# Causal mask added by VectorE in PSUM instead of by a product, the value halves added by VectorE, and another first weight load

## The chip, the cores and the metric

The kernel runs on one core of one Trainium2 chip. The metric is the device time of one execution in microseconds (us): the median of the runs of a kernel. The notes below call the engines PE (TensorE), DVE (VectorE), ACT (ScalarE), POOL (GpSimd) and SP (SyncE, which issues nearly all DMAs). PEld is TensorE's weight load.

## What is computed

One inference step of a hybrid streaming encoder layer for 1024 new frames of one stream (the prompt) and 32 frames of another that has 512 cached frames. Width 1024, 8 heads of 64, feed-forward width 4096, everything in float32.

```python
def _fox_attend(q, k, v, cq, ck, q_pos, k_pos):
    s = jnp.einsum('bqhd,bkhd->bhqk', q, k).astype(jnp.float32) * ATTN_SCALE
    bias = jnp.swapaxes(cq, 1, 2)[:, :, :, None] - jnp.swapaxes(ck, 1, 2)[:, :, None, :]
    mask = k_pos[None, :] <= q_pos[:, None]
    s = jnp.where(mask, s + bias, NEG_INF)
    p = jax.nn.softmax(s, axis=-1)
    return jnp.einsum('bhqk,bkhd->bqhd', p.astype(v.dtype), v)

u, q, k, v, logf, gc, ga = _in_proj(xp, w_in[l], b_f[l])        # one combined projection
y_conv = _conv_branch(u_ext, w_dw[l], b_dw[l], ln_conv_g[l], ln_conv_b[l], w_conv_out[l])
o_attn = _fox_prompt(q, k, v, logf)                             # blocks of 128 queries
# tail: two gated branches, w_o, LN, feed-forward with relu squared, LN
x1 = _layer_norm(DN_ALPHA * x + mix, ln1_g, ln1_b)
h = jnp.square(jax.nn.relu(jnp.einsum('btd,df->btf', x1, w_up)))
return _layer_norm(DN_ALPHA * x1 + jnp.einsum('btf,fd->btd', h, w_down), ln2_g, ln2_b)
```

## The kernel before

**Products.** Float32 operands are split into a high and a low part (`xh`, `xl`, `whi`, `wlo`), and each product is three: high by high, high by low, low by high. ACT copies the high part into the format that TensorE takes, DVE (in the attention stage POOL, for weights) subtracts it from the original to get the low part.

**Stages.** A first stage projects x to GLU, v, q, k and six of sixteen gate blocks. Then comes the attention, then the two output projections (`ps_yc`, `ps_yo`), `w_o` with a layer norm, and the feed-forward, which takes more than half of the time. Engines PE, DVE, ACT and POOL run their instructions in the order in which the program writes them. SP's order is made by the framework from the same program.

**The start.** `x_stream` loads the first weight block `raw` in halves and x in twelve pieces `xr` of two rows of 128 each (four pieces for each third of the frames). ACT turns them into `whi` and `xh`, DVE makes `wlo` and `xl`. The first block of products, `ps_glub`, goes through all high by high and high by low products in the order of the rows of x and then through the products with `wlo`. Small products that nobody reads (`ps_warm`, from `keep_warm`) run ahead of it and between its first products.

**Attention.** The work is a list of units: eight prompt heads of eight rows (a row is a block of 128 queries, named r = 0 to 7, that sees (r + 1) x 128 keys), and four cached units for the other stream between them. The loop runs a pipeline over these units. In iteration i PE makes the scores of unit i (`scores`, tile `ps_s`), the value products of unit i-3 (`values`, tile `ps_pv`, only at odd r, for two rows at once) and the transposes of unit i-2 (`turn`, tile `ps_tr`). DVE takes the negated maximum `mn` of the new scores (line 961), the reciprocal of the sum of unit i-1, normalises `p` of unit i-1 (line 231) and subtracts the high half from the transposed block (`tl`, unit i-2). ACT copies the high half `th`, and makes the exponential of the scores. There are two buffers for scores.

The mask of the diagonal block is the last product of a score: weights `ident_b` (an identity), moving operand `mask_b` (0 or a very large number, in bfloat16), both slices of the tile `bfs`. After the value products `fold` adds the two halves of the partitions (the parts from the high and the low half of v), and splits the result for the next stage; ACT copies both halves, POOL adds, casts and subtracts:

```python
act(a, pv[0:DH, :parts * n], AF.Copy)
act(b, pv[DH:P, :parts * n], AF.Copy)
tt(a, a, b, ADD, "pool")
```

**What sets the order.** While it writes the program, a planner (class `Issue`) keeps a model of each engine's time. `fill` is called ahead of the scores, transposes and value products: as long as the model says that their inputs aren't ready, and while a quota lasts, it puts in a step of other work (six products of one of the ten remaining gate blocks `ps_g`, or of the first `ps_yc` blocks). The quota begins at 16 steps and grows by 1.7 with each unit; there are 132 steps in all. Other work (`service`) is put in where the model says that it is due. The planner's costs for each instruction stand in the methods of `Issue`.

Of the kernel before, what the change touches and what calls it, by code (L numbers as in the profile page):

```python
# [267 lines left out]
def hybrid_layer(ctx: ExitStack, tc, io):  # L268
# [31 lines left out]
    eps = const.tile([P, 1], F32, name="eps")  # L300
    nc.gpsimd.memset(eps, EPS)
    tiny = const.tile([P, 1], F32, name="tiny")
    act(tiny, eps, AF.Sigmoid)

    def par(name, j):
        return prm[:, PRM[name] + j:PRM[name] + j + 1]
# [17 lines left out]
    class Weights:  # L324
# [1 line left out]
            self.raw, self.parts, self.taken, self.done, self.halves = [], [], 0, 0, 0  # L326
            self.engine, self.limit = "dve", NWO + 1

        def load(self):
            i = len(self.raw)  # L330
            held["raw"] += 1
            self.raw.append(ring.tile([P, RW // 2], F32, tag="raw", bufs=RAWB, name=f"raw{i}"))
            w = plan[i // 2]
            n = w.shape[1] // 2
            dma(self.raw[i][:, :n], w[:, i % 2 * n:(i % 2 + 1) * n])

        def split(self):
            i = self.halves
# [154 lines left out]
    with pool("conv") as pv_, pool("a") as pa, pool("pa", space=PSUM) as psa:  # L493
# [6 lines left out]
        def x_stream():  # L500
            raw = []

            def issue():
                i = len(raw)
                if i < 4 * NCH:
                    r = pa.tile([P, 2, CH], F32, tag="xr", bufs=XB, name=f"xr{i}")
                    dma(r, io["x"][2 * (i % 4):2 * (i % 4) + 2, :, chunks[i // 4]].rearrange("k p t -> p k t"))
                    raw.append(r)

            W.load()  # L510
            issue()
            issue()
            W.load()
            for _ in range(XB - 2):
                issue()
                if len(raw) == 4:
                    W.load()
                    W.load()
            W.split()
            for i in range(4 * NCH):  # L520
                if i == 1:
                    W.split()
                    W.load()
                    W.load()
                yield [raw[i]]
                cs = chunks[i // 4]
                for n in range(2):
                    k = 2 * (i % 4) + n
                    act(xh[k][:, cs], raw[i][:, n, :], AF.Copy)
                    tt(xl[k][:, cs], raw[i][:, n, :], f32(xh[k][:, cs]), SUB)  # L530
                xin.append(i)
                for _ in range((0, 1, 1, 2)[i] if i < 4 else 1):
                    issue()
# [6 lines left out]
        def keep_warm(n):  # L540
            for _ in range(n):
                nc.tensor.matmul(ps_warm, lhsT=warm[:, :P], rhs=warm, start=True, stop=True)
# [41 lines left out]
        def glu(kind, j, c):  # L584
            ps = bank(f"glu{kind}{j}")[:, :CH]
            if (kind, j) not in glu_w:
                glu_w[kind, j] = W.take()
            if (kind, j, c) == ("b", 0, 0):

                terms = on_x(glu_w[kind, j], c)  # L590
                for k, (wh, _, h, l) in enumerate(terms):
                    mm(ps, wh, h, k == 0, False)
                    mm(ps, wh, l, False, False)
                    keep_warm({1: 5, 3: 2}.get(k, 0))
                    I.service()
                for k, (_, wl, h, _) in enumerate(terms):
                    mm(ps, wl, h, False, k == KD - 1)
                I.service()
            else:
                dense(ps, on_x(glu_w[kind, j], c))  # L600
            if kind == "b":
                sig[j, c] = pa.tile([P, CH], F32, tag="sig", bufs=4, name=f"sig{j}_{c}")
                act(sig[j, c], ps, AF.Sigmoid)
            elif c < 2:
                tt(u[j][:, HIST + c * CH:HIST + (c + 1) * CH], ps, sig[j, c], MUL)
            else:
                e = SEQ - 2 * CH
                tt(u[j][:, HIST + 2 * CH:HIST + SEQ], ps[:, :e], sig[j, c][:, :e], MUL)
                tt(u[j][:, UE - DEC:UE], ps[:, e:], sig[j, c][:, e:], MUL)
                dma(io["conv_p"][:, j, :], u[j][:, SEQ:SEQ + HIST])  # L610
                dma(io["conv_d"][:, j, :], u[j][:, UE - HIST:UE])
# [209 lines left out]
    with pool("b") as pb, pool("pb", space=PSUM) as psb:  # L821
# [151 lines left out]
        def fold(pv, n, tag, outs, parts=1, into=None):  # L973
# [1 line left out]
            at = 0 if into is None else into[0]  # L975
            pr = slice(at, at + DH)
            a, b = (pb.tile([P, 256], F32, tag=x, bufs=1, name=f"{x}_{tag}")[pr, :parts * n] for x in ("oa", "ob"))
            act(a, pv[0:DH, :parts * n], AF.Copy)
            act(b, pv[DH:P, :parts * n], AF.Copy)
            tt(a, a, b, ADD, "pool")  # L980
            if parts > 1:
                tt(a[:, :n], a[:, :n], a[:, n:], ADD, "pool")
                a = a[:, :n]
# [14 lines left out]
        class Rows:  # L998
# [5 lines left out]
            def scores(self):  # L1004
                k1, k2, q1, q2, _ = self.ops
                n, tag = self.n, f"{self.h}_{self.r}"
                ps = psb.tile([P, SEQ], F32, tag="s", bufs=2, name=f"ps_s_{tag}")
                qc = slice(self.r * P, (self.r + 1) * P)
                I.fill(k1, k2, q1, q2, ps)
                for a in range(0, n, 512):  # L1010
                    w = min(512, n - a)
                    mm(ps[:, a:a + w], q1[:, qc], k1[:, a:a + w], True, False)
                    mm(ps[:, a:a + w], q2[:, qc], k2[:, a:a + w], False, a + w < n)
                mm(ps[:, n - P:n], ident_b, mask_b, False, True)
                self.sm = softmax_a(ps[:, :n], n, tag)

            def weigh(self):
# [941 lines left out]
```

## Time and profile before

| | |
|---|---|
| median of 3 runs | 1446.77 us (1445.07 to 1447.04) |
| profiled execution, its own time | 1445.13 us |
| its span, first to last instruction | 1443.0 us |
| mean granted TensorE clock over the span | 0.997 of 2.4 GHz |
| PE busy | 1427.9 us, 99% |
| DVE busy | 1121.0 us, 78% |
| ACT busy | 679.1 us, 47% |
| POOL busy | 124.5 us, 9% |
| attention on PE | from 334 to 572 us of the span |

Times within the trace count from the start of the span. A product is shown with a modelled end: products overlap, and the distance from one start to the next is what a product takes of PE. So PE's busy share can't tell whether PE is at its peak, and the starts are what to read.

### The profile page before, as it was taken

Reading aid. Unit: us, or ns where it says so; the run is one execution under the profiler, and the core shown is the slowest. Engines: PE = TensorE matmul, PEld = TensorE weight load, DVE = VectorE, ACT = ScalarE, POOL = GpSimd, SP = SyncE. Lnnn points to the kernel's source line nnn. Section 1 sums busy time; section 2 is a strip of 40 time slices with the busy share of each in tenths; the row PEclk is TensorE's granted clock in tenths of the full one; section 3 lists DMA queues with packets and bytes.
Section 4 is the critical chain, followed back from the end, with each engine's and each line's share of the span. In section 5 each row is a group of like instructions: output and inputs, shape, how many; then the busy total and the mean of one; then the engine's idle time right before and its main releaser. Section 6 shows DMA issues by size and latency. Waiting matters only on the chain.

```text
span 1443.0 us, 28013 instructions
## 1 busy us (share of the span) xinstructions
PE 1427.9 (99%) x10643; PEld 1406.3 (97%) x10643; DVE 1121.0 (78%) x1927; ACT 679.1 (47%) x1426; POOL 124.5 (9%) x183
## 2 busy tenths in 40 slices
PE   9999999999999999999999999999999999999996
PEld 8999999999999999999999999999999999999996
DVE  6999899875666555756697888889876799889668
ACT  5113433455656556533245666676657323322134
POOL 0000000023455533000000000000000000000000
PEclk9999999999999999999999999999999999999998
DMA  7125454278455557425243348766689999894212
GB/s 247 48 61 160 159 171 167 85 244 233 120 150 147 155 146 260 152 93 182 85 138 120 131 152 295 249 241 230 228 283 342 340 321 330 270 324 179 67 45 77
DMA packets 157441, 267.91 MB, mean 186 GB/s; under 512 B 22680, under 2 KB 81272, under 8 KB 157308
## 3 DMA queue, kind: packets, MB, share of 16 engines
q1 hardware_dynamic: 156492, 264.24, 55.0%
q0 software_dynamic: 544, 1.59, 0.5%
q8 instruction: 84, 1.38, 0.4%
q14 instruction: 49, 0.40, 0.1%
q10 hardware_dynamic: 272, 0.29, 0.1%
HBM read 168.29 MB, written 97.74 MB: 184 GB/s over the span
## 4 chain that ended last, share of the span: by engine, by line
PE 97%; DVE 1%; ACT 0%; DMA 0%; issue 0%; SPq 0%; DVEq 0%
PE ps_u L206 18%; PE ps_d L206 17%; PE ps_g L206 13%; PE ps_o L206 6%; PE ps_dn L206 6%; PE ps_up L206 5%; PE ps_v L206 4%; PE ps_yc L206 3%; PE ps_k L206 3%; PE ps_glua L206 3%; PE ps_q L206 3%; PE ps_glub L206 3%; PE ps_yo L206 3%; PE ps_s L206 3%; PE ps_pv L206 2%; PE ps_tr L210 2%
## 5 line engine op out<-in xcount | busy, mean ns | idle before, releaser
L235 DVE SCALAR_TENSOR_TENSOR ca<-u,prm,ca 128x1086 f32<-128x1086 f32 x120 | 161.8, 1348 | 2.4
L206 PE MATMUL ps_g<-xh,whi 128*128 128x352 f32 x384 | 131.8, 343 | 0.0
L218 ACT ACTIVATE swhi<-s 128x512 fp32r<-128x512 f32 x100 | 61.9, 624 | 148.2 <-DVE s L227 139.8
L206 PE MATMUL ps_g<-xh,wlo 128*128 128x352 f32 x384 | 123.8, 322 | 0.0
L206 PE MATMUL ps_g<-xl,whi 128*128 128x352 f32 x384 | 121.5, 322 | 0.0
L206 PE MATMUL ps_u<-tl,swhi 128*128 128x264 f32 x416 | 118.4, 285 | 0.0
L206 PE MATMUL ps_u<-th,swhi 128*128 128x264 f32 x416 | 118.2, 284 | 0.0
L206 PE MATMUL ps_u<-th,swlo 128*128 128x264 f32 x416 | 118.2, 284 | 0.0
L218 ACT ACTIVATE whi<-raw 128x512 fp32r<-128x512 f32 (+1 forms) x120 | 69.7, 624 | 68.6 <-PE ps_glua L206 21.8
L227 DVE TENSOR_TENSOR tl<-ps_tr,th 128x512 fp32r<-128x512 f32 (+2 forms) x96 | 51.5, 553 | 60.1 <-ACT th L218 59.4
L206 PE MATMUL ps_d<-hu_h,swhi 128*128 128x264 f32 x480 | 93.0, 285 | 0.0
L206 PE MATMUL ps_d<-hu_l,swhi 128*128 128x264 f32 x480 | 92.8, 285 | 0.0
L218 ACT ACTIVATE r<-r 128x528 f32<-128x528 f32 (+1 forms) x120 | 73.9, 615 | 37.8 <-DVE r L227 35.5
L227 DVE TENSOR_TENSOR r<-r,ps_u 128x528 f32<-128x528 f32 x91 | 62.7, 701 | 29.5 <-PE ps_u L206 29.5
L227 DVE TENSOR_TENSOR wlo<-raw,whi 128x512 fp32r<-128x512 f32 (+1 forms) x100 | 64.9, 687 | 23.5 <-ACT whi L218 21.6
L206 PEld LDWEIGHTS ps_u<-th,swhi 128*128 128x128 f32 x416 | 78.3, 188 | 0.0
L206 PEld LDWEIGHTS ps_u<-th,swlo 128*128 128x128 f32 x416 | 78.3, 188 | 0.0
L206 PEld LDWEIGHTS ps_u<-tl,swhi 128*128 128x128 f32 x416 | 78.2, 188 | 0.0
L227 POOL TENSOR_TENSOR acc<-acc,lnrest 128x288 f32<-128x288 f32 x4 | 3.0, 796 | 856.7 <-ACT lnrest L218 856.7
L206 PEld LDWEIGHTS ps_d<-hu_h,swhi 128*128 128x128 f32 x480 | 74.6, 189 | 0.3 <-issue 0.2
L206 PEld LDWEIGHTS ps_d<-hu_l,swhi 128*128 128x128 f32 x480 | 74.6, 189 | 0.0
L206 PEld LDWEIGHTS ps_g<-xh,whi 128*128 128x128 f32 x384 | 72.7, 189 | 0.8
(424 smaller groups left out, 5005.5 us busy)
## 6 DMA issues: line engine op xcount, KB each, us to landing
h_s<-sp SPq DMA_DIRECT2D x84, 528.0 KB
raw<-in_w_in_dram SPq DMA_DIRECT2D x64, 256.0 KB
hu_h<-h_s SPq DMA_DIRECT2D x30, 528.0 KB
hu_l<-h_s SPq DMA_DIRECT2D x30, 528.0 KB
sraw<-in_w_up_dram SPq DMA_DIRECT2D x52, 256.0 KB
hu<-h_s SPq DMA_DIRECT2D x24, 528.0 KB
sraw<-in_w_ds_dram SPq DMA_DIRECT2D x48, 256.0 KB
g_s<-gt SPq DMA_DIRECT2D x48, 176.0 KB
```

Of the source, the lines that this page charges most:

```text
L206: self.nc.tensor.matmul(ps, lhsT=w, rhs=x, start=start, stop=stop)
L210: self.nc.tensor.transpose(ps, x, ident)
L218: self.nc.scalar.activation(out, in_, func, **kw)
L227: (self.nc.vector if eng == "dve" else self.nc.gpsimd).tensor_tensor(out, a, b, op)
L235: self.nc.vector.scalar_tensor_tensor(out, a, s, b, op0, op1)
```

## The change

1. In `Rows.scores` the mask is no product any more. The second product of each piece closes the accumulation, and DVE adds `mask_b` to the last 128 columns of the scores in PSUM, ahead of the reduction. 64 products leave PE, 64 additions of 128 x 128 come to DVE. The cached units keep their mask product.
2. In `fold` ACT copies only the lower half `b`, and DVE adds the upper half, read from PSUM, to it. 36 copies leave ACT, 36 additions move from POOL to DVE.
3. The first weight half is issued on ACT's DMA queue, and the dummy activation that loads ACT's table for the sigmoid comes behind it. All other loads stay on SP.
4. In the first stage the second half of the first weight block is split after two pieces of x instead of one, and the two loads behind it move with it.
5. Between the first products there are 3 small warming products instead of 7.

```diff
-    act(tiny, eps, AF.Sigmoid)
...
-        def load(self):
+        def load(self, queue=None):
...
-            dma(self.raw[i][:, :n], w[:, i % 2 * n:(i % 2 + 1) * n])
+            dma(self.raw[i][:, :n], w[:, i % 2 * n:(i % 2 + 1) * n], queue)
...
-            W.load()
+            W.load(nc.scalar)
+            act(tiny, eps, AF.Sigmoid)
...
-                if i == 1:
+                if i == 2:
...
-                    keep_warm({1: 5, 3: 2}.get(k, 0))
+                    keep_warm({1: 2, 3: 1}.get(k, 0))
...
-            act(a, pv[0:DH, :parts * n], AF.Copy)
             act(b, pv[DH:P, :parts * n], AF.Copy)
-            tt(a, a, b, ADD, "pool")
+            tt(a, pv[0:DH, :parts * n], b, ADD)
...
-                    mm(ps[:, a:a + w], q2[:, qc], k2[:, a:a + w], False, a + w < n)
-                mm(ps[:, n - P:n], ident_b, mask_b, False, True)
+                    mm(ps[:, a:a + w], q2[:, qc], k2[:, a:a + w], False, True)
+                tt(ps[:, n - P:n], ps[:, n - P:n], mask_b, ADD)
```

Since the planner's times change, its filling steps in the attention move. Outside the start and the attention the order of all engines stays as it was, and the 132 steps stay inside the attention.

On DVE, in the second head: the iteration that makes the scores of row 4 and the one after it. `mn` is the reduction, `rs` the reciprocal, `p` the normalising, `tl` the low half of the transposed block, `oa` the sum of the halves. Before:

```order
L961 TENSOR_REDUCE mn_4_4177<-ps_s_4_4171 128x1
L239 RECIPROCAL rs_3_4156<-rs_3_4156 128x1
L231 TENSOR_SCALAR p_3_4155<-p_3_4155,rs_3_4156 128x512
L227 TENSOR_TENSOR tl_2_0_4208<-ps_tr_2_0_4209,th_2_0_4207 128x3x128
L961 TENSOR_REDUCE mn_5_4223<-ps_s_5_4217 128x1
L239 RECIPROCAL rs_4_4180<-rs_4_4180 128x1
L231 TENSOR_SCALAR p_4_4179<-p_4_4179,rs_4_4180 128x640
L227 TENSOR_TENSOR tl_2_0_4208<-ps_tr_3_0_4228,th_2_0_4207 128x4x128
```

After:

```order
L227 TENSOR_TENSOR ps_s_4_4185<-ps_s_4_4185,bfs 128x128
L961 TENSOR_REDUCE mn_4_4191<-ps_s_4_4185 128x1
L239 RECIPROCAL rs_3_4170<-rs_3_4170 128x1
L227 TENSOR_TENSOR oa_0_4226<-ps_pv_0_4221,ob_0_4227 64x256
L231 TENSOR_SCALAR p_3_4169<-p_3_4169,rs_3_4170 128x512
L227 TENSOR_TENSOR tl_2_0_4237<-ps_tr_2_0_4238,th_2_0_4236 128x3x128
L227 TENSOR_TENSOR ps_s_5_4246<-ps_s_5_4246,bfs 128x128
L961 TENSOR_REDUCE mn_5_4252<-ps_s_5_4246 128x1
L239 RECIPROCAL rs_4_4194<-rs_4_4194 128x1
```

The mask's addition stands ahead of each reduction; `oa`, which reads the value product and ACT's copy `ob`, stands ahead of the normalising of row 3 and of `tl` of row 2.

On PE, in the third head: from the scores of row 5 to the transposes of row 3. Before:

```order
L206 MATMUL ps_s_5_4596<-k_2_4079,q_2_4080 128x512
L206 MATMUL ps_s_5_4596<-k_0_3563,q_0_3565 128x512
L206 MATMUL ps_s_5_4596<-k_2_4079,q_2_4080 128x256
L206 MATMUL ps_s_5_4596<-k_0_3563,q_0_3565 128x256
L206 LDWEIGHTS bfs
L206 MATMUL ps_s_5_4596<-bfs 128x128
L210 MATMUL ps_tr_3_0_4607<-ident,p_3_4534 128x128 x4
L206 MATMUL ps_g_2_4621<-xh_139,whi_3518 128x352
```

After:

```order
L206 MATMUL ps_s_5_4644<-k_2_4091,q_2_4092 128x512
L206 MATMUL ps_s_5_4644<-k_0_3559,q_0_3561 128x512
L206 MATMUL ps_s_5_4644<-k_2_4091,q_2_4092 128x256
L206 MATMUL ps_s_5_4644<-k_0_3559,q_0_3561 128x256
L206 MATMUL ps_g_0_4579<-xh_144,whi_3672 128x352
L206 MATMUL ps_g_0_4579<-xl_152,whi_3672 128x352
L206 MATMUL ps_g_0_4579<-xh_144,wlo_3673 128x352
L206 MATMUL ps_g_0_4579<-xh_145,whi_3672 128x352
L206 MATMUL ps_g_0_4579<-xl_153,whi_3672 128x352
L206 MATMUL ps_g_0_4579<-xh_145,wlo_3673 128x352
L210 MATMUL ps_tr_3_0_4655<-ident,p_3_4575 128x128 x4
```

The product with `bfs` and its weight load are gone, and a filling step of six gate products, which stood behind the transposes, now stands ahead of them.

On ACT, at the start of the program. Before:

```order
L218 ACT_TABLE_LOAD
L218 ACTIVATE tiny<-eps 128x1
L218 ACTIVATE whi_210<-raw_186 128x512
L218 ACTIVATE xh_139<-xr_188 128x352
L218 ACTIVATE xh_140<-xr_188 128x352
L218 ACTIVATE whi_210<-raw_192 128x512
L218 ACTIVATE xh_141<-xr_190 128x352
L218 ACTIVATE xh_142<-xr_190 128x352
L218 ACTIVATE xh_143<-xr_194 128x352
```

After:

```order
L201 DMA raw_185<-in_w_in_dram 128x512
L218 ACT_TABLE_LOAD
L218 ACTIVATE tiny<-eps 128x1
L218 ACTIVATE whi_210<-raw_185 128x512
L218 ACTIVATE xh_138<-xr_188 128x352
L218 ACTIVATE xh_139<-xr_188 128x352
L218 ACTIVATE xh_140<-xr_190 128x352
L218 ACTIVATE xh_141<-xr_190 128x352
L218 ACTIVATE whi_210<-raw_192 128x512
```

The first DMA is issued by ACT ahead of its table load, and the second half of `whi` comes behind the fourth row of x instead of the second.

## Rows read from the trace of the kernel before

**Rows 1.** The page: span, busy time by engine, and the chain by engine.

```profile
span 1443.0 us, 28013 instructions
...
PE 1427.9 (99%) x10643; PEld 1406.3 (97%) x10643; DVE 1121.0 (78%) x1927; ACT 679.1 (47%) x1426; POOL 124.5 (9%) x183
...
PE 97%; DVE 1%; ACT 0%; DMA 0%; issue 0%; SPq 0%; DVEq 0%
```

**Rows 2.** Busy time in the attention: stretch, length, PE, PEld, DVE, ACT, POOL, clock, DMA.

```profile
334.00:572.00 238.00, 237.00 (x1656) 223.23 (x1656) 147.66 (x316) 147.74 (x370) 106.84 (x145) 1.00 0.58 168
```

**Rows 3.** Instructions that read the mask's tile: count, ns min/median/max, first and last start.

```profile
L206 PE MATMUL ps_s<-bfs x64: 229/230/233, 334.5 to 559.3; 128*128 128x128 bf16 x64
```

**Rows 4.** Timeline of PE, a mask with gate products behind it: start, length.

```profile
338.87 0.23 PE L206 MATMUL ps_s<-bfs 128*128 128x128 bf16 x1
338.91 0.41 PE L206 MATMUL ps_g<-xh,whi 128*128 128x352 f32 x1
339.16 0.32 PE L206 MATMUL ps_g<-xl,whi 128*128 128x352 f32 x1
339.32 0.32 PE L206 MATMUL ps_g<-xh,wlo 128*128 128x352 f32 x1
```

**Rows 5.** Timeline of PE, a mask with transposes behind it.

```profile
341.43 0.23 PE L206 MATMUL ps_s<-bfs 128*128 128x128 bf16 x1
341.49 0.61 PE L210 MATMUL ps_tr<-ident,p 128*128 128x128 f32 x4
```

**Rows 6.** Groups by form in the attention, DVE: busy us, mean ns, idle before.

```profile
L227 DVE TENSOR_TENSOR tl<-ps_tr,th 128x512 fp32r<-128x512 f32 x48 | 32.4, 686 | 27.5 <-ACT th L218 27.5
...
L227 DVE TENSOR_TENSOR tl<-ps_tr,th 128x256 fp32r<-128x256 f32 x16 | 6.6, 414 | 1.2 <-ACT th L218 1.2
...
L227 DVE TENSOR_TENSOR tl<-ps_tr,th 128x128 fp32r<-128x128 f32 x16 | 4.6, 288 | 19.0 <-ACT th L218 18.9
```

**Rows 7.** Instructions on the sum of the halves, ns min/median/max.

```profile
L218 ACT ACTIVATE oa<-ps_pv x32: 363/378/382, 340.6 to 572.0; 64x256 f32<-64x256 f32 x32
L227 POOL TENSOR_TENSOR oa<-oa,ob x32: 723/728/738, 341.4 to 572.9; 64x256 f32<-64x256 f32 x32
```

**Rows 8.** Waits in the attention: who on whom, us in total, times, longest.

```profile
DVE tl L227 <- ACT th L218: 59.4, 41, 3.1
...
PEld ps_s L206 <- ACT p L218: 1.1, 2, 0.9
```

**Rows 9.** Timeline of all engines in the second head, rows 1 to 5.

```profile
365.63 0.49 DVE L231 TENSOR_SCALAR p<-p,rs 128x512 f32<-128x512 f32 x1
...
366.53 0.38 ACT L218 ACTIVATE ob<-ps_pv 64x256 f32<-64x256 f32 x1
...
366.99 0.63 PE L210 MATMUL ps_tr<-ident,p 128*128 128x128 f32 x4
...
369.46 0.68 DVE L227 TENSOR_TENSOR tl<-ps_tr,th 128x512 fp32r<-128x512 f32 x1
...
370.31 0.28 PE L206 MATMUL ps_pv<-th,v 128*128 128x256 f32 x1
```

**Rows 10.** Timeline of the start, all engines, with idle time before and its releaser.

```profile
0.74 0.40 SPq L201 DMA_DIRECT2D raw<-in_w_in_dram  x1
...
1.19 4.11 PE L542 MATMUL ps_warm<-warm 128*128 128x256 bf16 x19 [1.19 <-DVE warm L537]
...
6.88 0.63 ACT L218 ACTIVATE whi<-raw 128x512 fp32r<-128x512 f32 x1 [0.93 <-DMA raw<-in_w_in_dram]
...
7.54 0.69 DVE L227 TENSOR_TENSOR wlo<-raw,whi 128x512 fp32r<-128x512 f32 x1 [0.98 <-ACT whi L218]
...
8.15 2.70 DVE L227 TENSOR_TENSOR xl<-xr,xh 128x352 fp32r<-128x352 f32 x6
```

**Rows 11.** Busy time at the start, columns as in rows 2, last two DMA share and GB/s.

```profile
1.00:2.00 1.00, 0.81 (x4) 0.58 (x5) 0.13 (x1) 1.00 (x1) 0.72 (x8) 1.00 0.15 33
...
3.00:3.50 0.50, 0.50 (x4) 0.32 (x3) 0.00 (x0) 0.00 (x0) 0.00 (x0) 1.00 0.96 246
```

## The prediction

> **What bounds the kernel now.** I read the page first: the chain that ended last is 97% PE, and PE is busy 99% of a span of 1443.0 us [rows 1]. A product's end is modelled, so the share alone proves little; the starts do. In the attention, from 334 to 572 us, PE is busy 237.0 of 238.0 us, DVE 147.7 (62%), ACT 147.7 and POOL 106.8 [rows 2]. The view of waits for that stretch says the same: the longest sum that PE or its weight load waits for another engine is 1.1 us, for ACT's exponentials [rows 8]. DVE waits 59.4 us there for ACT's high halves. So PE is the bound, the others have room, and PE work that goes away is gained, as long as what takes its place on DVE doesn't make PE wait. The start is another thing: its chain goes through the first DMAs, ACT and DVE [rows 10].
>
> **The change part by part.**
>
> *64 mask products off PE.* The trace shows a length of 230 ns for each [rows 3], but that is a modelled end; I take starts. Where gate products come behind the mask, the next one starts 0.04 us after it, but the one behind that comes 0.25 us later (338.91 to 339.16), where the usual distance is 0.16 (339.16 to 339.32) [rows 4]. So mask and delay take 0.04 + 0.09 = 0.13 us. Where transposes come behind it, they start 0.06 us after it [rows 5]; with a bit of delay I take 0.07. In the timeline 41 masks are followed by a wider product and 23 by transposes (one of each kind in [rows 4, 5]): 41 x 0.13 + 23 x 0.07 = 5.3 + 1.6 = **6.9 us**. Bounds: the distance to the next start alone, 41 x 0.04 + 23 x 0.06 = 3.0, and 64 x 0.13 = 8.3. I take 6.9, since the long distance behind a mask repeats in the rows and belongs to no other work.
>
> *64 additions on DVE.* No row has DVE write to PSUM. The nearest is `tl` with 128 columns out of PSUM, 288 ns [rows 6]: 64 x 0.29 = 18.4 us of DVE. Of the 288 ns only (686 - 288) / 384 x 128 = 133 are columns, 155 are paid for each instruction, so narrow additions are dear. The Trainium skill says this too (VectorE: DVE Perf Modes, section "The TRN2 errata"): VectorE pays a fixed extra for each instruction and TensorE doesn't, and its advice is 512 and more columns, which speaks against the change. By its formula the additions would take 64 x (120 + 128) / 0.96 ns = 16.5 us, an estimate near the rows' 18.4.
>
> *36 additions to DVE, 36 copies off ACT, 36 additions off POOL.* 32 are 256 wide: 0.41 us each by `tl` of that width [rows 6], 13.2 us; with four of 128 columns 14.4. ACT loses 0.38 each, POOL 0.73 each [rows 7]; both are off the chain, so that gains nothing itself. But ACT's high halves `th` come 0.38 us sooner behind a value product.
>
> DVE goes from 147.7 to about 147.7 + 18.4 + 14.4 = 180.5 us in a stretch of about 231: 78%. It stays below PE. What counts is its order. `oa` makes DVE wait for the value product and for ACT's copy, and behind it stand the normalising of the next row and `tl`, for both of which PE waits.
>
> *Is the new wait covered?* Take the second head, rows 1 to 5 [rows 9]. ACT's copy `ob` can start 0.40 us sooner than at 366.53, since the copy before it is gone: it ends at 366.51. Then `oa`, 0.41, to 366.95, and the normalising of row 3, 0.49, to 367.4. Before, that ran at 365.63. The transposes of row 3 stood at 366.99, so they would wait 0.4 us and a bit. One filling step of six gate products (6 x 0.16 = 0.96 us) covers this, and the changed order has one there: over the eight heads 9 steps stand ahead of these transposes, where there was 1, and 18 ahead of the value products of rows 2 and 3, where there were 9. Next, `tl` of row 3 ends at 370.14 and PE's product that reads it begins at 370.31: 0.17 us of room. Ahead of it come a mask addition and whatever is left of the delay, 0.3 to 0.7 us, and here too the filling has grown by one step per head. The steps are the same 132, only moved, so as a cover they cost nothing. If they weren't there, the delay would show.
>
> The filling doesn't hit exactly: today it leaves waits, of which the largest sum is 1.1 us [rows 8]. With a longer chain and 68 units I take **1.5 us** more of waits, bounds 0 (no more than now) and 4 (about half a microsecond per head).
>
> *The start.* SP issues the first weight half, two pieces of x, the second half: that DMA lands at 6.88, after ACT has been idle for 0.93 us, and DVE idle for 0.98 us until 7.54; then DVE works without a pause through 2.70 us of `xl` [rows 10]. With ACT issuing the first half, all that SP issues comes 0.46 us sooner (0.40 and the gap). With the split moved back, the rows 2 and 3 of x can be done in the idle hole: 2 x 0.48 = 0.96 us of DVE work comes out of the row of work behind 7.54. At best 1.4 us together. Against it: the DMA engines are 96% busy from 3.0 us on, but only 15% between 1 and 2 [rows 11], so the early issue fills what was empty, while later pieces wait for bytes. The Trainium skill has this rule (DMA: Bandwidth & Descriptors, section "Issuing engines are not separate DMA queues"): another issuing engine saves issue time only, since all share 16 engines; by it the DMA's part is at most the 0.46. I take **0.8 us** for the start, bounds -0.3 (the first half shares the engines with x and lands later) and 1.4. The four warming products that go lay in PE's idle time; they gain nothing, and their price, if the clock falls, is a rival below.
>
> *Sum.* 6.9 + 0.8 - 1.5 = 6.2 us. The profiled execution took 1445.13 us, 2.1 more than its span; the sum would bring it to 1438.9. It lies 1.6 below the median, so the median 1446.77 becomes **1440.6**. A difference under 0.2%, 2.9 us, can't be told from none here.
>
> **The rivals.**
>
> *A mask costs PE only its own slot.* If the 0.09 us behind the mask belongs to the change to the next weights and stays, 3.0 are gained, not 6.9: 1446.8 - 3.0 - 0.8 + 1.5 = 1444.5, no difference. For it: the trace shows what stands behind a mask only with the mask in place. Against: the starts add up to more time with a mask than without [rows 4]. The Trainium skill's formula for TensorE (VectorE: DVE Perf Modes, same section), 6 cycles and one per column, would give 56 ns, or 64 x 0.056 = 3.6 us, an estimate near this rival; the trace's 0.13 is more than twice that. Chance 0.08.
>
> *The filling runs out.* Behind a cached unit PE must wait for the loads of the next head's k and q. In the changed order only 4 filling steps stand between the first cached unit's scores and the next head's, where there were 8, so PE arrives up to 4 x 0.96 = 3.8 us sooner. If the loads don't come sooner as well, and the three other cached units lose a step's worth, up to 6.7 us are waited. Half of that gives 1440.6 + 3.4 = 1444.0, just no difference. Chance 0.07.
>
> *DVE's order becomes the bound.* Each pair of rows brings DVE 2 x 0.29 + 0.41 = 0.99 us and the wait for ACT's copy. If filling doesn't cover it, PE stands still in all 32 pairs. It needs 7.7 / 32 = 0.24 us a pair to eat the gain, and 0.33 to be slower by 0.2%. With 0.4, 12.8 us are lost: 1446.8 - 7.7 + 12.8 = 1451.9, slower. For it: rooms of 0.17 us as in [rows 9], and DVE at 78%. Against: 59.4 us in which DVE only waits for ACT's high halves, which come sooner, and the moved filling. Chance 0.09.
>
> *The clock falls at the start.* The 19 warming products take 4.11 us [rows 10], 0.216 each for 256 columns, which is 1.2 GHz; later gate products of 352 columns run at 0.16, which is 2.4. With four fewer between the first products the clock might fall back. If PE ran at 1.2 GHz for as long as it did at first, about 3.9 us, it would lose 1.9: 1442.5, still faster. Chance 0.05.
>
> **How the numbers follow.** Forecast 0.66, with 1440.6; its own bounds, from 6.9 and 0.8 at their best, go down to 1437.5. Clock 0.05 (faster). Better than the bounds 0.05 (DVE and ACT free each other: no new wait, and fewer than now). The cheap mask 0.08 and the filling 0.07: within 0.2%. DVE's order 0.09: slower. So faster 0.76, same 0.15, slower 0.09. The range goes from 1437.5 to 1446.0: it takes in both cases of no difference with their spread, and leaves out the slower rival and the 0.05 below.
>
> **What would show it.** Right: in the attention PE has 64 products fewer, its last value product of the last head ends about 6 us sooner counted from the first score, and DVE's busy time there is near 180 us. The mask's addition takes 0.26 to 0.32 us. At the start the last `xl` of the first third ends near 10.0 us instead of 10.85. PE's waits for `p`, `tl` or k stay under 5 us in the attention. Wrong: PE idle ahead of `ps_tr` or `ps_pv` with DVE as releaser in every head (DVE's order), PE idle ahead of a head's first `ps_s` behind cached units (filling), or a distance of 0.25 us still standing behind the scores (cheap mask). Should the first gate products behind the warming run at twice 0.16 us, the clock fell.

## The result and the profile after

The changed kernel takes 1447.79 us (median of 21 executions) beside 1445.77 for the kernel before, measured together with it. The ratio is 1.0014, with a 95% interval of 1.0008 to 1.0021: slower by about 2 us. One execution of the changed kernel that took 5662.76 us is left out of the ratio. The forecast was 1440.6, and its range ended at 1446.0.

The page of the changed kernel, in the parts of [rows 1]:

```profile
span 1445.7 us, 27892 instructions
...
PE 1423.5 (98%) x10575; PEld 1404.2 (97%) x10575; DVE 1148.7 (79%) x2027; ACT 668.7 (46%) x1390; POOL 106.3 (7%) x147
...
PE 95%; DVE 2%; DMA 1%; ACT 1%; issue 0%; POOL 0%; SPq 0%; DVEq 0%; ACTq 0%; POOLq 0%
```

PE has less to do and still ends later: its share of the chain fell from 97 to 95%. The attention, with the columns of [rows 2], from its first score to the product behind its last value product:

```profile
333.82:574.50 240.68, 232.61 (x1589) 221.02 (x1588) 174.78 (x415) 137.09 (x333) 89.06 (x110) 1.00 0.56 165
```

PE was busy for all but 1.0 us of 238 before; now 8.1 us of 240.7 are idle. Behind the attention both kernels need 871.33 us, so the whole difference lies in the attention and the start.

I read PE by its starts, as in the prediction. I count a product as late where its start follows the start before it by over 60 ns more than the median distance for the same forms around it. "PE's waits" below is the sum of what is over the median, and "the attention's length" runs from the first score to the first start behind the last value product.

| span of the profiled execution | before | after | difference | forecast |
|---|---|---|---|---|
| first score starts at | 334.31 | 333.82 | -0.49 | -0.8 |
| attention's length | 237.39 | 240.53 | +3.14 | -5.4 |
| of it PE's waits | 3.4 | 14.1 | +10.7 | +1.5 |
| of it all else | 234.0 | 226.5 | -7.5 | -6.9 |
| behind the attention | 871.33 | 871.33 | 0 | 0 |

The waits went wrong, far more than the masks' price. How the rise divides between the two depends on how waits are counted: this count goes by the shapes of products alone, and "all else" is only what it leaves. The profile's own idle time of PE grows by 7.1 us (1.0 to 8.1). The section on the experiments reads the masks' price from the starts themselves.

Who waits for whom in the attention (us, times, longest), beside [rows 8]:

```profile
DVE oa L227 <- ACT ob L218: 35.6, 27, 3.0
...
DVE tl L227 <- ACT th L218: 4.4, 5, 1.3
...
PEld ps_tr L210 <- DVE oa L227: 3.5, 4, 1.0
PEld ps_str L210 <- DVE oa L227: 3.3, 4, 0.8
PEld ps_tr L210 <- DVE tl L227: 3.3, 7, 0.9
...
PE ps_tr L210 <- DVE oa L227: 2.5, 4, 0.7
PE ps_str L210 <- DVE oa L227: 2.4, 4, 0.6
```

DVE waited 59.4 us for ACT's high halves before, now 4.4. It still has room, 66 us of the 240.7, but much of it has moved: DVE now waits 35.6 us for ACT's copy `ob`, ahead of `oa`, and what stands behind `oa` in its order waits with it. PE now waits for `oa`, which it had nothing to do with before. One of eight such places (the expectations below speak of nine), the timeline of all engines:

```profile
403.67 0.62 PE L210 MATMUL ps_tr<-ident,p 128*128 128x128 f32 x4
403.93 0.38 ACT L218 ACTIVATE ob<-ps_pv 64x256 f32<-64x256 f32 x1 [2.39 <-PE ps_pv L206]
...
404.42 0.42 DVE L227 TENSOR_TENSOR oa<-ps_pv,ob 64x256 f32<-64x256 f32 x1 [0.90 <-ACT ob L218]
...
404.89 0.33 PE L210 MATMUL ps_tr<-ident,p 128*128 128x128 f32 x1 [0.59 <-DVE oa L227]
```

Value products and transposes share two PSUM buffers (tag `tr`). The first group of transposes takes one, and the second group needs the one of the value product, which is only free when `oa` has read it. In the kernel before, a filling step stood between the two groups at each of these eight places, and the changed kernel has none there. The same place before (row 4 of the third head):

```profile
396.74 0.62 PE L210 MATMUL ps_tr<-ident,p 128*128 128x128 f32 x4
...
397.12 0.41 PE L206 MATMUL ps_g<-xh,whi 128*128 128x352 f32 x1
...
398.17 0.27 PE L210 MATMUL ps_tr<-ident,p 128*128 128x128 f32 x1
```

The addition of the mask and `oa` themselves, in the form of [rows 3, 7]:

```profile
L227 DVE TENSOR_TENSOR ps_s<-ps_s,bfs x64: 276/289/300, 334.2 to 563.1; 128x128 f32<-128x128 f32 x64
...
L227 DVE TENSOR_TENSOR oa<-ps_pv,ob x32: 407/417/419, 341.9 to 575.0; 64x256 f32<-64x256 f32 x32
```

The start, beside [rows 10]:

```profile
0.74 0.43 ACTq L201 DMA_DIRECT2D raw<-in_w_in_dram  x1
...
7.00 0.62 ACT L218 ACTIVATE whi<-raw 128x512 fp32r<-128x512 f32 x1
...
7.64 0.69 DVE L227 TENSOR_TENSOR wlo<-raw,whi 128x512 fp32r<-128x512 f32 x1
...
8.43 1.93 DVE L227 TENSOR_TENSOR xl<-xr,xh 128x352 fp32r<-128x352 f32 x4
```

Two of six `xl` moved ahead of 7.64, and the last of the third ends at 10.36 instead of 10.85.

### The profile page after: what moved, and what is told of

Its sections match the earlier page's. It is cut to its first block, busy times and chain, and to the rows that moved or that the text cites. A ratio compares the mean times of both kernels' runs of the same rounds, so it can differ in the third digit from the quotient of the medians.

```text
span 1445.7 us, 27892 instructions
## 1 busy us (share of the span) xinstructions
PE 1423.5 (98%) x10575; PEld 1404.2 (97%) x10575; DVE 1148.7 (79%) x2027; ACT 668.7 (46%) x1390; POOL 106.3 (7%) x147
## 4 chain that ended last, share of the span: by engine, by line
PE 95%; DVE 2%; DMA 1%; ACT 1%; issue 0%; POOL 0%; SPq 0%; DVEq 0%; ACTq 0%; POOLq 0%
PE ps_u L206 18%; PE ps_d L206 17%; PE ps_g L206 12%; PE ps_o L206 6%; PE ps_dn L206 6%; PE ps_up L206 5%; PE ps_v L206 4%; PE ps_k L206 3%; PE ps_glua L206 3%; PE ps_q L206 3%; PE ps_glub L206 3%; PE ps_yc L206 3%; PE ps_yo L206 3%; PE ps_pv L206 2%; PE ps_s L206 2%; PE ps_tr L210 2%
## 5 line engine op out<-in xcount | busy, mean ns | idle before, releaser
L206 PE MATMUL ps_g<-xh,whi 128*128 128x352 f32 x384 | 128.0, 333 | 0.0
L206 PEld LDWEIGHTS ps_g<-xl,whi 128*128 128x128 f32 x384 | 71.9, 188 | 1.0
L206 PEld LDWEIGHTS ps_g<-xh,wlo 128*128 128x128 f32 x384 | 72.1, 188 | 0.0
```

The source lines that it names most:

```text
L206: self.nc.tensor.matmul(ps, lhsT=w, rhs=x, start=start, stop=stop)
```

## The experiments

**Parts of the change.** Theory A: the buffer held by `oa` makes PE wait. B: DVE's longer order does. C: a mask product costs PE less than thought.

`e1_mask`: the mask on DVE alone.

```diff
-                    mm(ps[:, a:a + w], q2[:, qc], k2[:, a:a + w], False, a + w < n)
-                mm(ps[:, n - P:n], ident_b, mask_b, False, True)
+                    mm(ps[:, a:a + w], q2[:, qc], k2[:, a:a + w], False, True)
+                tt(ps[:, n - P:n], ps[:, n - P:n], mask_b, ADD)
```

> Kernel before with the mask's addition on DVE as its only change (part 1). Theory A (held buffer): the time after went into PE's second group of transposes, which waits for the PSUM buffer that the value product holds until DVE has added the halves; the mask part alone should then gain most of its 6.9 us: 4 to 7 us faster than before. Theory B (DVE's chain): the 64 additions ahead of the reductions make tl late and use up the filling steps; then this part alone gains under 3 us. Theory C (cheap mask): the 64 products cost PE only 3 us; then 1 to 3 us faster at most, with no new waits on PE.

`e2_fold`: the addition of the halves alone.

```diff
-            act(a, pv[0:DH, :parts * n], AF.Copy)
...
-            tt(a, a, b, ADD, "pool")
+            tt(a, pv[0:DH, :parts * n], b, ADD)
```

> Kernel before with only the halves of the value products added by DVE (part 2). Theory A: slower than before by 3 to 7 us, with PE waiting ahead of the second group of transposes for DVE's sum. Theory B: the 14 us of DVE work here alone cost 0 to 2 us, the waits come only with the mask's additions on top.

`e3_start`: parts 3 to 5 alone.

```diff
-    act(tiny, eps, AF.Sigmoid)
...
-            W.load()
+            W.load(nc.scalar)
+            act(tiny, eps, AF.Sigmoid)
...
-                if i == 1:
+                if i == 2:
...
-                    keep_warm({1: 5, 3: 2}.get(k, 0))
+                    keep_warm({1: 2, 3: 1}.get(k, 0))
```

> Kernel before with only the changes at the start (parts 3 to 5). All theories: 0.5 us faster, as the first score of the changed kernel stood 0.49 us sooner in its trace (333.82 against 334.31); anything outside 0 to 1 us would mean that the attention's order hangs on the start.

`e4_nomask`: no mask at all for the prompt's rows.

```diff
-                    mm(ps[:, a:a + w], q2[:, qc], k2[:, a:a + w], False, a + w < n)
-                mm(ps[:, n - P:n], ident_b, mask_b, False, True)
+                    mm(ps[:, a:a + w], q2[:, qc], k2[:, a:a + w], False, True)
```

> Kernel before with the mask products of the prompt rows left out and nothing in their place: the prompt's attention is then not causal within the diagonal block. It measures what 64 mask products cost PE. By the rows of before (0.13 and 0.07 us each) 6.9 us faster; by theory C 3 us faster. PE's waits should stay at the 4 to 5 us of before.

| | time, us | ratio to before | interval | attention | PE's waits |
|---|---|---|---|---|---|
| before | 1445.6 | | | 237.4 | 3.4 |
| e1_mask | 1447.6 | 1.0015 | 1.0006 to 1.0025 | 238.3 | 12.2 |
| e2_fold | 1449.4 | 1.0025 | 1.0016 to 1.0035 | 241.5 | 6.4 |
| e3_start | 1445.1 | 0.9994 | 0.9985 to 1.0003 | 237.4 | 3.4 |
| e4_nomask | 1444.5 | 0.9990 | 0.9982 to 0.9999 | 235.6 | 9.5 |

The mask on DVE alone costs 2.0 us and the new `fold` alone 3.8. For `fold` that is the size that theory A asked for, but only two of its waits are of the kind shown above (0.76 us each). Two others of 1.4 us each come behind normalisings of 2.2 us that ran beside POOL, an event of the kind shown last.

The decisive one is `e4_nomask`. It puts nothing on DVE and holds no buffer longer, and yet PE's waits grow, by 6.1 us in this count. The count is too high there: going by shapes alone, it takes in distances that stand at every such place once the mask is gone. Counted by names and shapes, with medians over all runs, the waits are 2.4 us before, 5.8 here, 8.8 in `e1_mask` and 11.5 in the changed kernel; PE's idle time in the profile is 1.0, 3.7, 5.6 and 8.1 us. Read straight from the starts (from a score's last product to the third product behind it, the mask not counted, medians of the same forms in both kernels), the 64 masks took about 5.0 us of PE. Of these only 1.8 are gained; 3.2 come back as waits. So for the mask neither A nor B is needed to lose most of the gain, and C explains it only in part. PE's waits in `e4_nomask` (us, times, longest):

```profile
PE ps_tr L210 <- DVE tl L227: 2.7, 4, 1.4
PE ps_str L210 <- ACT ob L218: 0.5, 1, 0.5
PE ps_tr L210 <- ACT ob L218: 0.5, 1, 0.5
```

Two of them stand, as the change's do, between two groups of transposes with no filling step left between them (0.64 us over the median each, for ACT's `ob`). The mask products had been a cover for the chain of DVE and ACT, and the filling that should take their place isn't there: in all four, as in before and after, the trace has 690 filling products in the attention.

**The held buffer.** `e5_after_sbuf`: the whole change, with ACT copying both halves.

```diff
+            act(a, pv[0:DH, :parts * n], AF.Copy)
             act(b, pv[DH:P, :parts * n], AF.Copy)
-            tt(a, pv[0:DH, :parts * n], b, ADD)
+            tt(a, a, b, ADD)
```

> The changed kernel, but ACT copies both halves of the value product and DVE adds them from SBUF, so that the PSUM buffer is free when ACT is done. Held buffer: the waits of some 0.76 us between two groups of transposes go, PE's waits fall from 14.1 to about 7 us, time 1441 to 1443.5 where the changed kernel took 1447.8. Filling too scarce: the chain through DVE is as long as before, other waits take their place, PE's waits stay over 11 us and the time stays within 1446 to 1449.

It took 1453.07 us, 1.0053 of before (1.0041 to 1.0065), with 18.6 us of waits, so A fails as the whole cause:

```profile
PE ps_tr L210 <- DVE tl L227: 4.3, 4, 2.1
PE ps_tr L210 <- ACT ob L218: 2.4, 5, 0.5
PE ps_str L210 <- ACT ob L218: 1.4, 3, 0.5
```

The regular waits come back with another name, at 0.64 us instead of 0.76, now for ACT's two copies. The rest is no clean test of A, since `oa` now reads only SBUF:

```profile
L227 DVE TENSOR_TENSOR oa<-oa,ob x32: 416/418/2609, 342.4 to 581.0; 64x256 f32<-64x256 f32 x32
```

One of them took 2.61 us and one 1.53 beside subtractions on POOL. PE's waits behind these two (1.5 and 2.2 us) and a stretch at a granted clock of 0.50 behind the second (547 to 550 us) make some 5 of the 18.6.

**More filling** (theory D: the supply of filling is too small). Two gate blocks moved from the first stage into the supply: 24 steps more.

```diff
-GA = 6
+GA = 4
```

> The changed kernel with four gate blocks in the first stage instead of six, so that 156 filling steps lie in the attention instead of 132. The work is the same. Filling too scarce: PE's waits in the attention fall from 14.1 us to under 7, time 1440 to 1443. Held buffer or DVE's order as a bound that filling can't cover: waits stay over 10 us, time within 1.5 us of the changed kernel's 1447.8.

> Control: the kernel before with 156 filling steps. Filling too scarce only where the change cut it: PE waits only 3.4 us before, so at most 2 us are to be had, time 1444 to 1446.5 beside 1445.8. If the shift of two gate blocks is good in itself, this gains as much as the changed kernel does from it.

> The kernel before without the 64 mask products of the prompt's rows and with nothing in their place, and with 156 filling steps. It leaves out the causal mask of the diagonal blocks. Filling too scarce: the products' whole price shows now, 6 to 8 us below the kernel before, 1438 to 1440, where without the added filling it was 1.2 us. If a mask product is cheap on PE (its slot alone), the gain stays under 3 us and the waits of PE are small in both.

| | time, us | ratio to before | attention | filling products in it | PE's waits |
|---|---|---|---|---|---|
| f2_before_ga4 | 1471.9 | 1.0182 | 236.7 | 690 | 2.7 |
| f3_nomask_ga4 | 1466.1 | 1.0144 | 238.4 | 730 | 5.9 |
| f1_after_ga4 | 1465.7 | 1.0138 | 253.2 | 786 | 11.7 |

All three times miss: the first stage doesn't get shorter by what left it. The windows from 200 to 330 us, the changed kernel first, then `f2_before_ga4`:

```profile
200.00:330.00 130.00, 130.00 (x804) 128.48 (x804) 107.13 (x140) 54.30 (x109) 10.96 (x17) 1.00 0.52 170
```

```profile
200.00:330.00 130.00, 111.13 (x675) 109.47 (x674) 104.54 (x136) 51.79 (x103) 12.46 (x19) 0.92 0.51 163
```

There the two blocks had been filling as well. What the runs do show is the demand: offered 24 steps more, the kernel before takes none into its attention, the one without masks 40 products, the changed one 96. At 0.16 us each that is 6.4 and 15.4 us. Counted without these products, the attention is 236.7, 232.0 and 237.8 us: with the filling there, the missing masks gain 4.7 us instead of 1.8. The 4.7 are close to the masks' price read from the starts.

The changed kernel's waits fall only by 2.4 us in the sum, but that hides two things. At all eight places shown above, a filling step stands between the groups again, and no such wait is left. Instead there are waits of 1.4, 1.4 and 0.7 us behind DVE instructions that POOL held up (a normalising of 2.18 us, a cast of 1.50), and after the last of them the granted clock was 0.50 to 0.55 from 511 to 514 us, which the count of late starts takes in with 1.4:

```profile
512.00:513.00 1.00, 1.00 (x5) 1.00 (x5) 0.96 (x3) 1.00 (x3) 1.00 (x3) 0.50 0.26 62
```

**Three buffers.** One PSUM buffer moved from the gate products to the ring.

```diff
...
-tag="tr", bufs=2
+tag="tr", bufs=3
...
-        return psb.tile([P, 512], F32, tag="acc", bufs=2, name="ps_" + name)
+        return psb.tile([P, 512], F32, tag="acc", bufs=1, name="ps_" + name)
```

> Control for the next three: the kernel before with three PSUM buffers instead of two for the ring that transposes and value products share, and one instead of two for the gate products (whose last block then goes through its thirds one after another). PE waited 3.4 us in the attention before, so three buffers can give at most that, and one gate buffer can cost a little: 1444 to 1449 beside 1445.8.

> The changed kernel with the three buffers. Held buffer: the waits of the second transposes for DVE's addition go (some 9 x 0.76 = 6.8 us), PE's waits in the attention fall from 14.1 to under 8, and the change now gains: 3 to 6 us under its control. Order of DVE's work as the bound: waits of this size stay and it is 0 to 4 us over its control, as with two buffers.

> The kernel before without the 64 mask products of the prompt's rows and with nothing in their place, with the three buffers. It leaves out the causal mask of the diagonal blocks. Held buffer: PE's waits stay under 5 us (9.5 with two buffers), and the products' price shows, 5 to 8 us under the control. Mask products cheap on PE: under 3 us, as with two buffers (1.2).

> The mask on DVE and the changed start, with the old fold (ACT copies both halves, POOL adds) and the three buffers. Held buffer: 4 to 7 us under the control, and the fastest of all if the control isn't over 1447. Otherwise the mask's addition itself keeps PE waiting: within 1.5 us of the control.

Inconclusive. The four took 1485.1, 1463.2, 1470.2 and 1476.1 us, with 26.3, 19.4, 22.8 and 32.7 us of waits, because the price of the one gate buffer is far above my 3 us. In the control:

```profile
PE ps_g L206 <- ACT gt L218: 14.2, 18, 2.3
PE ps_tr L210 <- DVE p L231: 3.6, 2, 2.8
```

PE no longer waits for `oa` in `g4_after_tr3`, but the differences between these four are in large part differences in gate waits.

**Padding instead of filling.** Now as many products without a reader as the planner asks for, in steps of two, and the real filling behind the attention. The attention's length is then what its own chain needs, with as much cover as the planner's model of the engines asks for.

```diff
+        def padding():
+            ps = bbank("pad")[:, :2 * P]
+            while True:
+                for _ in range(2):
+                    mm(ps, ident_b, bfs[:, :2 * P], True, True)
+                yield None
+
+        I.filler.insert(0, [padding(), None])
-        I.quota = Q0
+        I.quota = 1e6
...
```

> The kernel before, but in the attention the filling is made of small products that nobody reads, as many as the planner asks for; all real filling steps follow behind the attention. So the attention's length on PE (first score to last value product) shows what the chain of its own work needs. Chain sets it: 225 to 238 us beside 237.4 before. PE sets it (the filling was in the way): under 215.

> The padded kernel without the 64 mask products of the prompt's rows and with nothing in their place (the causal mask of the diagonal blocks is left out). Chain sets the length: within 2.5 us of the padded kernel before, with more padding. PE sets it: 5 to 7 us shorter.

> The padded kernel with the mask added by DVE. Chain sets the length: 7 to 16 us longer than the padded kernel before (up to 64 x 0.288 = 18.4 us if each addition lies on the chain). PE sets it: 5 to 7 us shorter.

> The padded kernel with the whole change. Chain sets the length: 10 to 18 us longer than the padded kernel before. PE sets it: 5 to 7 us shorter.

The padding products, first scores and last value products of the four in this order (count, ns, first and last start):

```profile
L206 PE MATMUL ps_pad<-bfs x904: 269/273/283, 318.1 to 550.9; 128*128 128x256 bf16 x181
...
L206 PE MATMUL ps_s<-k,q x192: 221/390/506, 333.1 to 540.7; 128*128 128x512 f32 x96, 128*128 128x128 f32 x32, 128*128 128x256 f32 x32, 128*128 128x384 f32 x32
...
L206 PE MATMUL ps_pv<-tl,v x160: 277/282/288, 338.1 to 552.8; 128*128 128x256 f32 x128, 128*128 128x128 f32 x32
```

```profile
L206 PE MATMUL ps_pad<-bfs x958: 269/273/288, 319.3 to 552.0; 128*128 128x256 bf16 x192
...
L206 PE MATMUL ps_s<-k,q x192: 221/389/504, 334.3 to 541.8; 128*128 128x512 f32 x96, 128*128 128x128 f32 x32, 128*128 128x256 f32 x32, 128*128 128x384 f32 x32
...
L206 PE MATMUL ps_pv<-tl,v x160: 277/282/288, 339.4 to 553.8; 128*128 128x256 f32 x128, 128*128 128x128 f32 x32
```

```profile
L206 PE MATMUL ps_pad<-bfs x1000: 269/273/286, 318.4 to 554.8; 128*128 128x256 bf16 x167
...
L206 PE MATMUL ps_s<-k,q x192: 221/390/504, 333.4 to 544.1; 128*128 128x512 f32 x96, 128*128 128x128 f32 x32, 128*128 128x256 f32 x32, 128*128 128x384 f32 x32
...
L206 PE MATMUL ps_pv<-tl,v x160: 274/282/389, 339.4 to 556.6; 128*128 128x256 f32 x128, 128*128 128x128 f32 x32
```

```profile
L206 PE MATMUL ps_pad<-bfs x1044: 269/273/286, 317.1 to 555.1; 128*128 128x256 bf16 x174
...
L206 PE MATMUL ps_s<-k,q x192: 221/388/494, 332.1 to 544.2; 128*128 128x512 f32 x96, 128*128 128x128 f32 x32, 128*128 128x256 f32 x32, 128*128 128x384 f32 x32
...
L206 PE MATMUL ps_pv<-tl,v x160: 274/282/384, 338.1 to 557.0; 128*128 128x256 f32 x128, 128*128 128x128 f32 x32
```

In every one 138 of the padding products lie ahead of the first score. One takes 0.109 us, from the group of 39 in a row ((4.42 - 0.27) / 38):

```profile
399.80 4.42 PE L206 MATMUL ps_pad<-bfs 128*128 128x256 bf16 x39
```

| | time, us | attention | padding products in it | their time | PE's waits |
|---|---|---|---|---|---|
| p1_before_pad | 1560.2 | 219.8 | 766 | 83.5 | 4.7 |
| p2_nomask_pad | 1560.6 | 219.6 | 820 | 89.4 | 6.6 |
| p3_mask_pad | 1562.9 | 223.3 | 862 | 94.0 | 5.5 |
| p4_after_pad | 1563.7 | 225.0 | 906 | 98.8 | 8.4 |

Without the masks the attention is as long as with them (-0.2 us), and 5.9 us of padding stand where they stood. That is the chain's reading, and PE's (5 to 7 us shorter) is out for this form. With the mask on DVE and the whole change it is 3.5 and 5.2 us longer, less than I expected; that much of DVE's 18.4 us still lies beside other waits is likely, but not shown. And 219.8 us is below my 225: with its real filling, 690 products at 0.16 or 110 us in steps of six, the kernel before is bound by PE's work after all, but with hardly a filling step to spare.

So the change raises what must be bridged by 15.3 us (83.5 to 98.8): 5.9 by the masks that go, 4.6 by the addition on DVE, 4.8 by `fold`. The filling is of a fixed amount. PE's waits in the real kernels rise by 6.1, 2.7 and 1.9 over the same steps (before, `e4_nomask`, `e1_mask`, after). With padding at no limit, all eight places are covered again, and no wait for `oa` is longer than 0.2 us. In the count of late starts 3.7 us more of waits stay with the change (8.4 over 4.7), but the profile shows no more idle time of PE, 4.0 us before and 3.3 with the change (length less PE's busy time; `p1_before_pad`, then `p4_after_pad`):

```profile
333.07:552.89 219.82, 215.84 (x1730) 183.89 (x1727) 148.06 (x316) 124.16 (x318) 79.94 (x125) 1.00 0.39 99
```

```profile
332.10:557.08 224.98, 221.70 (x1805) 193.15 (x1803) 172.09 (x415) 115.38 (x283) 63.06 (x90) 1.00 0.38 97
```

So, by the idle time, enough cover takes the extra waits away, and the 5.2 us of length are the chain's. In sum the real filling, 110 us, is more than the 98.8 us of padding. What falls short is then rather its steps of six products and where the quota lets them stand; that is argued, not shown.

**Smaller filling steps.** The same filling in steps of two products (`j7_after_fine`, the whole change) and of three (`j3_mask_start_fine`, the mask and the start), with the quota scaled up.

```diff
...
-            if s % (8 if low else 6) == (7 if low else 5) and s < n - 1:
+            m = 8 * lump[0] // 6 if low else lump[0]
+            if s % m == m - 1 and s < n - 1:
...
```

> The changed kernel with filling steps of two products instead of six in the attention, and three times as many of them: the same work in smaller steps. Filling used up in steps too large: PE's waits in the attention fall from 14.1 us to under 8, and the time to 1439 to 1444 beside 1447.8. DVE's order as a bound that no filling covers: waits stay over 10 us and the time at 1446 to 1449.

> The mask on DVE and the changed start with the old fold, and filling steps of three products, twice as many. Filling used up in steps too large: PE's waits fall from the 12.2 us of the mask alone to under 6, time 1437 to 1442, the fastest of all. Otherwise 1445 to 1448.

They took 1446.46 us (1.0006, 0.9997 to 1.0015) and 1445.50 (0.9999, 0.9990 to 1.0007), with 11.1 and 10.5 us of waits: in the right direction, and far from the 1439 to 1444 and 1437 to 1442 expected. In the first, seven of the eight places are covered again, and two waits behind instructions that POOL held up (1.7 us at 397, 1.4 at 501) are part of what is left. In the second, much of what was left is one such event, shown last. No version that keeps the mask beat the kernel before by more than the measurement can tell; the start alone is nearest to it.

## Why the prediction was wrong

- **64 mask products at 0.13 and 0.07 us, 6.9 us of PE: too high by some 2 us.** By the starts with and without them (before, `e4_nomask`) a mask took 0.12 us with gate products behind it, 0.07 where the score's last piece is 128 wide, and 0.00 to 0.05 with transposes behind it; about 5.0 in all. The row that gave 0.13 [rows 4] is of the 128 wide kind: without the mask the second gate product there still starts 0.22 us after the first, so the long distance is not the mask's alone. The cheap-mask rival (3.0 us) was partly right. By the count of waits in the table above it would be 7.5, but that is a remainder.
- **64 additions on DVE, bounded by `tl` of 128 columns: right,** 289 ns for 288. `oa` at 0.41: right, 417 ns. DVE's 180 us: 174.8.
- **"PE is the bound, ... and PE work that goes away is gained": wrong in its second half.** PE's 99% was 127 us of its own products and waits and 110 us of other stages' products that the planner had put into the chain's gaps. Where the changed kernel lost a filling step, none was left to take its place. A product taken off PE leaves a gap that it had covered: in the padded pair 5.9 us of padding took the masks' place, and the stage was no shorter.
- **"The steps are the same 132, only moved, so as a cover they cost nothing": this is the step that failed.** A step that moves ahead of the transposes of row 3 is missing elsewhere: eight of the new waits stand where a step was taken away, and they are gone where steps were added. The extra waits were put at 1.5 us, bounds 0 to 4, and measured 10.7 (7.1 as PE's idle time in the profile). I had the numbers: I saw that scores behind cached units had fewer steps ahead of them, and made it a rival of 3.4 us at four places instead of a price on the whole sum.
- **Where the waits would be: half right.** I followed `oa` to the normalising and to `tl`. I missed that `oa` also holds the PSUM buffer of the second group of transposes, the most regular of the new waits. Eight, seven of them 0.76 us over the median and one 0.90, make 6.2 of the 14.1. In `e5_after_sbuf`, with DVE out of that hold, there are eight such waits again, of 0.64 us, for ACT.
- **The rival of DVE's order** had its point of slowness at 0.33 us for each of 32 pairs; measured were 10.7 / 32 = 0.33, or 0.22 by PE's idle time. The size fits, the mechanism only in part: waits of 3.2 us came without any work on DVE.
- **The start, -0.8 us: right in sign, 0.5.** The clock rival didn't come: the first gate products run at 0.16 us again. The granted clock is 1.00 there in both kernels, also while the warming products run at 0.21, so it doesn't show the 1.2 GHz that I read from their starts.
- **The range** was worked out loosely: with 8.3, 1.4 and 1.5 the best case is 1438.6, without new waits 1437.1, not 1437.5. It makes no difference to the outcome.

Shown is that masks on PE were a cover, and that the most regular of the new waits, 6.2 us, stand where the change took a filling step away: with more filling, with padding and, but for one, with smaller steps they are gone. How the rest divides is less sharp. In the sum of late starts more filling took 2.4 us away and smaller steps 3.0; of what stayed, a good part are single events in which POOL holds DVE up. Not run was the change with the planner's own prices put right: its formula for DVE gives 209 ns for the mask's addition and 339 for `oa`, where 289 and 417 were measured, and better prices might place the same steps better. A clean run with more filling and nothing else changed wasn't found either: the two blocks came out of a first stage that needed them, and the third buffer out of the gate products.

## What to carry to other kernels

An engine that is 99% busy because a planner pads it with other work is at a balance, not at a bound with free room beside it. Before work is taken off it, ask what that work had been covering, and whether any padding is left. Replacing the padding by products without a reader tells in one run how long the stage's own chain is and how much cover it asks for. And an added reader of a shared buffer is costed by who takes the buffer next, not only by what is queued behind it on its engine.

## What the runs showed of the hardware

One collision of DVE and POOL cost PE twice. It is not the only one. In the attention, DVE instructions that take over 0.1 us more than the median of their form do so by 6.4 us in sum before, 6.3 in `e4_nomask`, 7.7 with the change and 12.4 in `j7_after_fine`; the first three are too close to explain the new waits. In `j3_mask_start_fine`, timeline and then windows (columns as in rows 2):

```profile
496.79 2.72 POOL L227 TENSOR_TENSOR wlo<-raw,whi 128x512 fp32r<-128x512 f32 x2 [2.41 <-ACT whi L218]
...
497.12 2.67 DVE L222 CAST sk<-ckr 128x512 fp32r<-128x512 f32 x2
...
499.71 1.08 DVE L231 TENSOR_SCALAR p<-p,rs 128x768 f32<-128x768 f32 x1
...
500.71 0.88 DVE L227 TENSOR_TENSOR tl<-ps_tr,th 128x512 fp32r<-128x512 f32 x2
...
501.45 1.33 PE L210 MATMUL ps_tr<-ident,p 128*128 128x128 f32 x6 [1.94 <-DVE tl L227]
```

```profile
499.00:501.00 2.00, 0.51 (x3) 0.07 (x1) 2.00 (x3) 1.32 (x4) 1.94 (x3) 1.00 0.63 189
501.00:502.00 1.00, 0.55 (x4) 0.56 (x5) 0.97 (x4) 0.00 (x0) 0.92 (x3) 0.86 0.50 148
502.00:503.00 1.00, 1.00 (x6) 1.00 (x5) 1.00 (x2) 0.61 (x2) 1.00 (x1) 0.50 0.31 81
```

The pair of casts took 2.67 us where one alone takes 0.41 to 0.42 in the changed kernel; here the longest single one is 1515 ns. POOL's two subtractions ran beside it. The Trainium skill (SBUF — State Buffer, section "SBUF: two separate sides") calls the port pair of DVE and GpSimd an exclusive lock, held for a whole instruction, on which the loser blocks; the trace agrees, with about 1.1 us lost on that cast. The normalising and `tl` come late behind it, and PE waits 1.94 us. Then the granted clock is at 0.50, that is 1.2 GHz, from 502 to 505 us, so about 1.5 us more are lost at half speed (an estimate: half of three us). The `ps_tr` wait and this make some 3.4 us, more than the difference under study. In `j7_after_fine` a wait of 1.7 us at 397 us left the clock at 1.00.
